# Seven-product pairs in the down-projection: a raw buffer of their own, loads two steps ahead in order, and another order of steps in the first pass

## The chip, the cores and the metric

The kernel runs on 1 core of one Trainium2 chip. The metric is device time in microseconds of one execution. The time before is 2037.37 us, the median of three runs (2033.04 to 2039.13).

## The reference, cut to what matters

The program is a two-layer decoder trunk on 256 tokens of width 2048: mixer and attention blocks, and in each layer a gated feed-forward block. The change touches the second matrix product of that block alone:

```python
def conv_ffn(h, w_up, cw, cb, w_down):
    a = h @ w_up                                  # 256 x 2048 @ 2048 x 11264
    ap = jnp.pad(a, ((0, 0), (CONV_W - 1, 0), (0, 0)))
    c = sum(ap[:, k:k + S] * cw[k] for k in range(CONV_W)) + cb
    gate, val = c[..., :D_FF], c[..., D_FF:]
    return (jax.nn.silu(gate) * val) @ w_down     # 256 x 5632 @ 5632 x 2048
```

All data is float32. TensorE multiplies a rounded type (fp32r), so each operand is split into a high part (`whi`, a rounded copy made by ScalarE) and a low part (`wlo`, the raw value less the high part, made by VectorE), and each block product is three matmuls: high by high, high by low, low by high.

## The kernel before, in words

**Groups and calls.** The 5632 hidden channels are taken in three groups of 2048, 2048 and 1536. For each of the first two groups of each layer, `gemm_seven` multiplies the hidden values of the group (2048 channels, 16 row blocks of 128) by the 2048 x 2048 piece of `w_down`. So `gemm_seven` runs four times, at 521 us, 780 us, 1482 us and 1743 us of the profiled execution.

**Passes and steps.** A call makes two passes, one for each 1024 output columns. A pass has eight steps; a step is a pair of row blocks, that is 1 MB of weights: 256 rows by 1024 columns, or four blocks of 128 x 512, b11 and b12 (the first 128 rows, left and right 512 columns), b21 and b22 (the second 128 rows). In the text steps are counted from 1 and pairs from 0, so before the change pair m stands at step m + 1 in both passes.

**Ordinary and seven-product pairs.** An ordinary pair makes 8 block products, 24 matmuls. Pairs 3 and 5 (`SEVEN`) use Winograd's form of Strassen's scheme and make 7 block products, 21 matmuls; they need four differences of weight blocks first: t1 = b12 - b11, t3 = b22 - b12, t2 = b22 - t1, t4 = b21 - t2. `differences(i, 0)` makes t1 and t3, `differences(i, 1)` makes t2 and t4. The sums of the other operand (`s7`) are made during the up-projection.

**What a step does on each engine.** `load` issues the DMAs on SP's queue into `raw` tiles of 512 KB each, of which there are 4. `prepare` makes `whi` and `wlo` of each part, by ScalarE and VectorE; an ordinary pair has 2 parts of 128 x 1024, a seven-product pair has four (before: [b11, b21] of 1024, b22 of 512, [t1, t2] and [t3, t4] of 1024). There are 4 `whi` and 4 `wlo` buffers, so a part can be made only when TensorE is through with the part that stands four parts ahead. `products` is the step's matmuls, in `three` (L290 to L292).

**Order.** Inside `gemm_seven` TensorE, ScalarE, VectorE and SP run in the order in which the code writes the instructions (`manual_schedule`); each engine takes its own queue in order and waits at the head of it. While step i is multiplied, the code writes: the first two differences of step i + 2 if that is a seven-product pair (with its load ahead of them), the parts of step i + 1 (with their load), the last two differences of step i + 2, the matmuls of step i, and up to three of the delayed additions that bring finished sums from the accumulation banks to the running total. After a seven-product pair's last step four such additions bring the Strassen sums together (four more in the three calls after the first, where the total already holds something), and four more follow each pass.

**First steps of a call.** VectorE still has work of the up-projection to finish when a call begins: two scalings, eight multiply-adds of the convolution (L828), two products `hv` and two splits `h`. They lie in its queue between the parts of the first steps.

## Time and profile before

| | |
|---|---|
| runs shown | 2033.04, 2039.13, 2037.37 us; median 2037.37 |
| the profiled execution | 2035.25 us in all, span 2033.5 us, granted TensorE clock 0.999 |
| TensorE busy | 2020.3 us, 99% of the span, 15394 matmuls |
| VectorE, ScalarE busy | 1493.2 us (73%), 1080.7 us (53%) |
| DMA | 64.7% of 16 engines' span on SP's queue, 192 GB/s of HBM traffic over the span |
| `gemm_seven`, matmuls of four calls | L290, L291 and L292, 496 each, 389 to 391 ns each, overlapped |

A matmul of 128 x 512 is shown as busy for 389 ns, but the next one starts 227 ns after it: they are pipelined. A stall of TensorE is therefore read from the starts of two following matmuls, less 0.23 us, rather than from idle time alone. In timelines a row gives start, length, engine, line and operation, then the idle time before it and what ended that.

### The profile page before, as it was taken

To read this page: it belongs to the slowest core of one execution; us is meant where nothing else is said; L and a number is where in the kernel's file an instruction comes from. 1 tells how busy PE (TensorE), PEld (TensorE's weight loads), DVE (VectorE), ACT (ScalarE), POOL (GpSimd) and SP (SyncE) were. 2 spreads that over 40 slices of the span, in tenths; PEclk is the share of its full clock that TensorE was granted. 3 is DMA by queue.
4 is the path that set the end of the run, shared out by engine and by line. 5 is a ranking of instruction groups with operands and counts; after the bars stand their busy time and mean duration, and the time that the engine had idled before them with its cause. 6 is when DMAs were issued, how large, how long until landed. Compare 5 with 4: busy or idle time off the path is not lost.

```text
span 2033.5 us, 37724 instructions
## 1 busy us (share of the span) xinstructions
PE 2020.3 (99%) x15394; PEld 1923.9 (95%) x15394; DVE 1493.2 (73%) x2064; ACT 1080.7 (53%) x1424; POOL 95.1 (5%) x131
## 2 busy tenths in 40 slices
PE   9999999999999999999999999999999999999998
PEld 8989999999889998899999999999988999889997
DVE  6866667767776777877789886777678667786675
ACT  6754644555545555445546674455544555544543
POOL 0000013000000000000052002200000000000000
PEclk9999999999999999999999999999999999999999
DMA  8675855666566665688665565578756666566654
GB/s 312 186 236 176 199 179 186 206 190 192 185 213 190 195 196 180 213 214 214 190 195 185 172 151 166 192 209 214 222 186 199 195 201 188 183 204 195 199 185 154
DMA packets 254013, 398.86 MB, mean 196 GB/s; under 512 B 65040, under 2 KB 71824, under 8 KB 253712
## 3 DMA queue, kind: packets, MB, share of 16 engines
q1 hardware_dynamic: 253264, 395.80, 64.7%
q8 instruction: 120, 1.97, 0.4%
q10 hardware_dynamic: 576, 0.66, 0.1%
q14 instruction: 53, 0.43, 0.1%
HBM read 388.01 MB, written 2.10 MB: 192 GB/s over the span
## 4 chain that ended last, share of the span: by engine, by line
PE 94%; DVE 3%; DMA 2%; issue 1%; ACT 1%; ACTq 0%; POOLq 0%; POOL 0%; DVEq 0%
PE ps L180 23%; PE ps L181 23%; PE ps L183 23%; PE ps L291 4%; PE ps L292 4%; PE ps L290 4%; PE ps L211 3%; PE ps L212 3%; PE ps L213 3%; DMA raw<-in_w_ffn_down 1%; DVE wlo L270 1%; DVE c L828 0%; ACT whi L269 0%; PE ps L714 0%; PE ps L767 0%
## 5 line engine op out<-in xcount | busy, mean ns | idle before, releaser
L144 DVE TENSOR_TENSOR wlo<-raw,whi 128x1024 fp32r<-128x1024 f32 (+1 forms) x544 | 664.3, 1238 | 396.2 <-issue 254.0
L143 ACT ACTIVATE whi<-raw 128x1024 fp32r<-128x1024 f32 (+1 forms) x544 | 569.4, 1054 | 574.1 <-PE ps L181 435.6
L180 PE MATMUL ps<-xhl,whi 128*128 128x256 f32 x3264 | 750.6, 276 | 0.0
L181 PE MATMUL ps<-xhl,whi 128*128 128x256 f32 x3264 | 750.2, 276 | 0.0
L180 PEld LDWEIGHTS ps<-xhl,whi 128*128 128x128 f32 x3264 | 612.6, 188 | 0.2
L181 PEld LDWEIGHTS ps<-xhl,whi 128*128 128x128 f32 x3264 | 612.6, 188 | 0.2
L183 PE MATMUL ps<-xhl,wlo 128*128 128x256 f32 x3264 | 403.2, 276 | 0.0
L183 PEld LDWEIGHTS ps<-xhl,wlo 128*128 128x128 f32 x3264 | 385.2, 188 | 0.0
L269 ACT ACTIVATE whi<-raw 128x1024 fp32r<-128x1024 f32 (+1 forms) x128 | 126.0, 1004 | 113.8 <-DMA raw<-in_w_ffn_down 45.8
L270 DVE TENSOR_TENSOR wlo<-raw,whi 128x1024 fp32r<-128x1024 f32 (+1 forms) x128 | 144.8, 1155 | 48.3 <-ACT whi L269 22.2
L291 PE MATMUL ps<-wlo,h 128*128 128x512 f32 x432 | 168.7, 391 | 2.5 <-DVE wlo L270 2.5
L290 PE MATMUL ps<-whi,h 128*128 128x512 f32 x432 | 168.4, 390 | 1.3 <-ACT whi L269 1.3
L292 PE MATMUL ps<-whi,h 128*128 128x512 f32 x432 | 168.2, 389 | 0.0
L828 DVE SCALAR_TENSOR_TENSOR c<-a,cT,c 128x255 f32<-128x255 f32 (+1 forms) x352 | 145.9, 477 | 0.0
L825 ACT ACTIVATE c<-a,cT 128x256 f32<-128x256 f32 x176 | 91.6, 591 | 77.4 <-DVE a L419 77.4
L180 PE MATMUL ps<-mainhl,whi 128*128 128x256 f32 x512 | 118.5, 278 | 0.0
L181 PE MATMUL ps<-mainhl,whi 128*128 128x256 f32 x512 | 118.0, 277 | 0.0
L291 PEld LDWEIGHTS ps<-wlo,h 128*128 128x128 f32 x432 | 81.1, 188 | 21.2 <-DVE wlo L270 4.4
L290 PEld LDWEIGHTS ps<-whi,h 128*128 128x128 f32 x432 | 81.1, 188 | 18.6 <-ACT whi L269 1.9
L292 PEld LDWEIGHTS ps<-whi,h 128*128 128x128 f32 x432 | 81.1, 188 | 16.8
L180 PEld LDWEIGHTS ps<-mainhl,whi 128*128 128x128 f32 x512 | 96.0, 188 | 0.1
L181 PEld LDWEIGHTS ps<-mainhl,whi 128*128 128x128 f32 x512 | 96.0, 188 | 0.1
(325 smaller groups left out, 2389.6 us busy)
## 6 DMA issues: line engine op xcount, KB each, us to landing
raw<-in_w_ffn_up SPq DMA_DIRECT2D x352, 512.0 KB, 4.2
raw<-in_w_ffn_down SPq DMA_DIRECT2D x176, 512.0 KB, 4.8
raw<-in_w_out SPq DMA_DIRECT2D x64, 512.0 KB, 4.9
raw<-in_w_in_a SPq DMA_DIRECT2D x56, 512.0 KB, 4.5
raw<-in_w_mem_kv SPq DMA_DIRECT2D x31, 512.0 KB, 5.3
raw<-in_w_in_b SPq DMA_DIRECT2D x16, 512.0 KB, 3.9
raw<-in_w_uq SPq DMA_DIRECT2D x12, 384.0 KB, 3.4
raw<-in_w_kv_a SPq DMA_DIRECT2D x8, 512.0 KB, 3.7
```

The costliest lines, as they stand in the source:

```text
L143: nc.scalar.activation(hi[:, :n], raw[:, :n], AF.Copy)
L144: nc.vector.tensor_tensor(lo[:, :n], raw[:, :n], hi[:, :n].bitcast(F32), ALU.subtract)
L180: mm(acc, wh, x[:, :S], start=first, stop=False)
L181: mm(acc, wh, x[:, S:], start=False, stop=False)
L183: mm(acc, wl, x[:, :S], start=False, stop=last)
L269: nc.scalar.activation(hi, raw, AF.Copy)
L270: nc.vector.tensor_tensor(lo, raw, hi.bitcast(F32), ALU.subtract)
L290: mm(acc, xh, wh, start=start, stop=False)
L291: mm(acc, xh, wl, start=False, stop=False)
L292: mm(acc, xl, wh, start=False, stop=stop)
L825: nc.scalar.activation(c[:, i, :], a[:, i, :], AF.Identity, scale=w(2), bias=w(3))
L828: nc.vector.scalar_tensor_tensor(o, a[:, i, : S - 2 + j], w(j), o, ALU.mult, ALU.add)
```

## The change

The seven-product pairs get a tile of their own, `raw7` (128 x 4 x 512, one buffer), and no longer use the four `raw` tiles. Their load is three DMAs in place of two: the first 128 rows with all 1024 columns (512 KB, 4 KB from each row), then two of 256 KB for b21 and b22. The tile holds b11, b12, b22, b21 in this order, so that t1 and t3 are one subtraction of 128 x 1024; t2 and t4 stay two of 128 x 512. The parts become b11 (512), [b22, b21] (1024), [t1, t3] (1024) and [t2, t4] (1024), and the products of the pair are ordered to use them in this sequence.

Loads are issued two steps ahead in the order of the steps, for all pairs. In the first pass the pairs are taken in the order 0, 1, 2, 4, 3, 6, 5, 7, so that the seven-product pairs stand at steps 5 and 7; in the second pass they stay at steps 4 and 6. Four delayed additions are allowed in a step in place of three. To make room in SBUF, masks, rotary tables and scratch squares move from a pool that lives through the whole program into one that ends before the last feed-forward block, and the transposition after the first layer uses `raw7` in place of a tile of its own.

```diff
-            prepare(0)
+            load(0)
+            load(1)
+            prepare(0)
             for i in range(len(steps)):
+                if i + 2 < len(steps):
+                    load(i + 2)
                 if seven(i + 2):
                     differences(i + 2, 0)
                 if i + 1 < len(steps):
                     prepare(i + 1)
                 if seven(i + 2):
                     differences(i + 2, 1)
-                now, later[:] = later[:3], later[3:]
+                now, later[:] = later[:4], later[4:]
                 products(i)
...
+ORDERS = ((0, 1, 2, 4, 3, 6, 5, 7), (0, 1, 2, 3, 4, 5, 6, 7))
...
         def load(i):
-            raws[i] = [self.raw_load(src(i, c)) for c in range(2)]
+            half, m = steps[i]
+            if not seven(i):
+                blocks[i] = [self.raw_load(src(i, c)) for c in range(2)]
+                return
+            raw = blocks[i] = self.tmp(sums, [P, 4, 512], "raw7", 1)
+            row = lambda j: self.rows(dn, half * 1024, 1024)(2 * m + j, 1).rearrange("p k (c n) -> p (k c) n", c=2)
+            nc.sync.dma_start(out=raw[:, 0:2, :], in_=row(0))
+            for c in range(2):
+                nc.sync.dma_start(out=raw[:, 3 - c, :], in_=row(1)[:, c, :])
 
         def differences(i, part):
+            raw = blocks[i]
             if part == 0:
-                load(i)
-                early[i] = [self.tmp(pool, [P, 4, S], "gate", 2).rearrange("p a s -> p (a s)") for _ in range(2)]
-            (b11, b21), (b12, b22) = ((raw[:, :512], raw[:, 512:]) for raw in raws[i])
-            (t1, t2), (t3, t4) = ((t[:, :512], t[:, 512:]) for t in early[i])
-            if part == 0:
-                sub(t1, b12, b11)
-                sub(t3, b22, b12)
-            else:
-                sub(t2, b22, t1)
-                sub(t4, b21, t2)
+                early[i] = [self.tmp(pool, [P, 4, S], "gate", 2).rearrange("p (a b) s -> p a (b s)", a=2) for _ in range(2)]
+                sub(early[i][0], raw[:, 1:3, :], raw[:, 0:2, :])
+                return
+            t13, t24 = early[i]
+            sub(t24[:, 0, :], raw[:, 2, :], t13[:, 0, :])
+            sub(t24[:, 1, :], raw[:, 3, :], t24[:, 0, :])
...
-            self.three(side[1], block(2 * m, 0), pick(one, 0), first, last)
-            self.three(out[0, 0], block(2 * m + 1, 0), pick(one, 1))
-            self.three(out[0, 1], s[3], pick(b22, 0))
-            self.three(side[5], s[0], pick(ta, 0), first, last)
-            self.three(side[6], s[1], pick(ta, 1), first, last)
-            self.three(side[7], s[2], pick(tb, 0), first, last)
-            self.three(out[1, 0], block(2 * m + 1, 1), pick(tb, 1))
+            self.three(side[1], block(2 * m, 0), pick(b11, 0), first, last)
+            self.three(out[0, 0], block(2 * m + 1, 0), pick(b2, 1))
+            self.three(out[0, 1], s[3], pick(b2, 0))
+            self.three(side[5], s[0], pick(t13, 0), first, last)
+            self.three(side[7], s[2], pick(t13, 1), first, last)
+            self.three(side[6], s[1], pick(t24, 0), first, last)
+            self.three(out[1, 0], block(2 * m + 1, 1), pick(t24, 1))
```

Two places show how the change moves instructions. The first is SP's queue in the first pass of the first call, from the load of the third step on. Before (`raw_757` and `raw_758` are pair 3, `raw_761` and `raw_762` pair 2, `raw_775` and `raw_776` pair 5, `raw_779` and `raw_780` pair 4):

```order
L262 DMA raw_757_6086<-in_w_ffn_down 128x2x512
L262 DMA raw_758_6088<-in_w_ffn_down 128x2x512
L262 DMA raw_761_6094<-in_w_ffn_down 128x2x512
L262 DMA raw_762_6096<-in_w_ffn_down 128x2x512
L262 DMA raw_775_6172<-in_w_ffn_down 128x2x512
L262 DMA raw_776_6174<-in_w_ffn_down 128x2x512
L262 DMA raw_779_6180<-in_w_ffn_down 128x2x512
L262 DMA raw_780_6182<-in_w_ffn_down 128x2x512
```

And the same place with the change (`raw_749` and `raw_750` are pair 2, then pair 4, pair 3 in `raw7`, pair 6, pair 5 in `raw7`, pair 7):

```order
L263 DMA raw_749_6050<-in_w_ffn_down 128x2x512
L263 DMA raw_750_6052<-in_w_ffn_down 128x2x512
L263 DMA raw_759_6090<-in_w_ffn_down 128x2x512
L263 DMA raw_760_6092<-in_w_ffn_down 128x2x512
L316 DMA raw7_765_6126<-in_w_ffn_down 128x1024
L318 DMA raw7_765_6126<-in_w_ffn_down 128x512 x2
L263 DMA raw_772_6167<-in_w_ffn_down 128x2x512
L263 DMA raw_773_6169<-in_w_ffn_down 128x2x512
L316 DMA raw7_782_6211<-in_w_ffn_down 128x1024
L318 DMA raw7_782_6211<-in_w_ffn_down 128x512 x2
L263 DMA raw_793_6253<-in_w_ffn_down 128x2x512
L263 DMA raw_794_6255<-in_w_ffn_down 128x2x512
```

The load of an ordinary pair no longer stands behind that of the seven-product pair that is multiplied after it; the load of the second seven-product pair now stands behind the parts of the first one, which hold the single `raw7`.

The second place is VectorE's queue in the second pass of the first call, from the parts of pair 3 (step 4) to the parts of pair 4 (step 5). Before:

```order
L270 TENSOR_TENSOR wlo_837_6461<-raw_826_6413,whi_836_6460 128x1024
L270 TENSOR_TENSOR wlo_839_6465<-raw_827_6415,whi_838_6464 128x512
L270 TENSOR_TENSOR wlo_841_6469<-gate_828_6417,whi_840_6468 128x1024
L270 TENSOR_TENSOR wlo_843_6473<-gate_829_6418,whi_842_6472 128x1024
L296 TENSOR_TENSOR gate_846_6504<-raw_845_6502,raw_844_6500 128x512
L296 TENSOR_TENSOR gate_847_6505<-raw_845_6502 128x512
L270 TENSOR_TENSOR wlo_851_6513<-raw_848_6508,whi_850_6512 128x1024
L270 TENSOR_TENSOR wlo_853_6517<-raw_849_6510,whi_852_6516 128x1024
```

With the change:

```order
L271 TENSOR_TENSOR wlo_836_6462<-raw7_826_6416,whi_835_6461 128x512
L271 TENSOR_TENSOR wlo_838_6466<-raw7_826_6416,whi_837_6465 128x1024
L271 TENSOR_TENSOR wlo_840_6470<-gate_827_6420,whi_839_6469 128x1024
L271 TENSOR_TENSOR wlo_842_6474<-gate_828_6421,whi_841_6473 128x1024
L297 TENSOR_TENSOR gate_844_6505<-raw7_843_6501 128x1024
L271 TENSOR_TENSOR wlo_847_6509<-raw_833_6457,whi_846_6508 128x1024
L271 TENSOR_TENSOR wlo_849_6513<-raw_834_6459,whi_848_6512 128x1024
```

The two first differences of pair 5 have become one, at the same place: behind the last part of pair 3 and ahead of both parts of pair 4. Their input, `raw7_843`, is the buffer that the first two rows read as `raw7_826`.

## The prediction

> **What bounds the kernel now.** I read the page first, then the waits of TensorE, then its timeline at those waits, then the chain that ends one of them.

> ```profile
> span 2033.5 us, 37724 instructions
> PE 2020.3 (99%) x15394; PEld 1923.9 (95%) x15394; DVE 1493.2 (73%) x2064; ACT 1080.7 (53%) x1424; POOL 95.1 (5%) x131
> ```

> TensorE is busy for 99% of the span, and the change takes no matmul away. It can gain only what TensorE loses in waits. Those for TensorE on this change's lines, summed over the whole run:

> ```profile
> PE ps L291 <- DVE wlo L270: 2.5, 4, 0.8
> PE ps L290 <- ACT whi L269: 1.3, 1, 1.3
> ```

> Five waits, all in the four calls of `gemm_seven`. Matmuls overlap, so the true loss is read from starts. TensorE's timeline at the fifth step of the first pass of each call:

> ```profile
> 541.88 0.39 PE L290 MATMUL ps<-whi,h 128*128 128x512 f32 x1
> 543.04 0.50 PE L291 MATMUL ps<-wlo,h 128*128 128x512 f32 x1 [0.76 <-DVE wlo L270]
> 543.37 0.39 PE L292 MATMUL ps<-whi,h 128*128 128x512 f32 x1
> ...
> 801.47 0.39 PE L290 MATMUL ps<-whi,h 128*128 128x512 f32 x1
> 802.22 0.50 PE L291 MATMUL ps<-wlo,h 128*128 128x512 f32 x1 [0.37 <-DVE wlo L270]
> ...
> 1503.01 0.40 PE L292 MATMUL ps<-whi,h 128*128 128x512 f32 x1
> 1504.69 0.49 PE L290 MATMUL ps<-whi,h 128*128 128x512 f32 x1 [1.28 <-ACT whi L269]
> 1505.94 0.50 PE L291 MATMUL ps<-wlo,h 128*128 128x512 f32 x1 [0.76 <-DVE wlo L270]
> ...
> 1764.71 0.40 PE L290 MATMUL ps<-whi,h 128*128 128x512 f32 x1
> 1765.71 0.50 PE L291 MATMUL ps<-wlo,h 128*128 128x512 f32 x1 [0.60 <-DVE wlo L270]
> ```

> The undisturbed distance of two starts is 0.23 us (front part), so the waits cost 1.16 - 0.23 = 0.93, 0.75 - 0.23 = 0.52, 1.45 + 1.02, and 0.77 us. The matmul after a wait starts 0.33 us on (543.04 to 543.37), which adds 0.10 to each call. Sum: 0.93 + 0.52 + 2.47 + 0.77 + 0.40 = **5.1 us**. What is late there, by the chain that ended last:

> ```profile
> 535.21 5.35 DMA raw<-in_w_ffn_down
> ...
> 541.76 1.23 DVE wlo L270
> 543.00 0.04 issue
> 543.04 0.50 PE ps L291
> ```

> Pair 4's first DMA is issued at 535.21 only, lands at 540.56, and its `wlo` is ready at 542.99, 0.05 us before TensorE starts. It was issued late because it stood on SP's queue behind pair 5's load.

> **The change part by part.** *Removed: the late load.* With loads in the order of the steps and pair 4 moved to step 4, an ordinary pair waits for its own `raw` tiles alone, which come free two ordinary pairs earlier. The step that comes fifth is now pair 3, whose `raw7` is empty at the start of a call, so its three DMAs go out directly behind pair 4's. VectorE's leftover of the up-projection is over by then:

> ```profile
> 524.20 3.23 DVE L828 SCALAR_TENSOR_TENSOR c<-a,cT,c 128x255 f32<-128x255 f32 x8
> ```

> It ends near 527.4, fourteen us ahead of the step that stalls. I take all 5.1 us as removed.

> *Added: a wait for the single `raw7`.* Pair 5 can be loaded only when the last reader of pair 3 in `raw7` is through, the `wlo` of [b22, b21]. Its first difference stands on VectorE ahead of both parts of the ordinary pair in between (step 6 of the first pass, step 5 of the second). If the load is late, those two `wlo` wait behind it, and TensorE waits for the first of them at its second matmul. That is eight places, two in each call. Timing of the second pass of the first call, before the change:

> ```profile
> 575.08 0.63 ACT L269 ACTIVATE whi<-raw 128x512 fp32r<-128x512 f32 x1 [1.52 <-PE ps L292]
> 577.85 1.06 ACT L269 ACTIVATE whi<-gate 128x1024 fp32r<-128x1024 f32 x1 [2.13 <-PE ps L292]
> 581.66 1.23 DVE L270 TENSOR_TENSOR wlo<-gate,whi 128x1024 fp32r<-128x1024 f32 x1 [1.49 <-ACT whi L269]
> 582.80 0.69 DVE L296 TENSOR_TENSOR gate<-raw,raw 128x512 f32<-128x512 f32 x1
> 584.01 2.35 DVE L270 TENSOR_TENSOR wlo<-raw,whi 128x1024 fp32r<-128x1024 f32 x2
> 585.30 0.47 PE L291 MATMUL ps<-wlo,h 128*128 128x512 f32 x1
> 585.62 0.39 PE L292 MATMUL ps<-whi,h 128*128 128x512 f32 x1
> ```

> The second part's `whi` starts at 575.08, when TensorE releases its buffer. The new second part is 1024 wide: 575.08 + 1.06 + 0.06 + 1.23 (the `wlo`) = 577.43, and SP issues at 577.45. Call D the time from there until the third DMA has landed. Then 0.10 until VectorE starts (a transfer landing at 540.56 was used at 540.66), 1.14 for the one difference of 1024 (the distance of two 1024-wide operations, 582.80 less 581.66), 1.23 for the `wlo`, 0.05 to TensorE: 2.52 us. TensorE wants it at 585.30. The stall is 577.45 + D + 2.52 - 585.30 = D - 5.33, and with the restart of 0.10, **D - 5.23**. With D below 5.2 VectorE would start the difference at 582.80, as now, and there is no stall: 582.80 + 1.14 + 1.23 + 0.05 = 585.22. The present 0.09 us (585.62 - 585.30 - 0.23) would go too; over the calls some 0.2 us.

> In the second passes of the three later calls additions to the total lie between:

> ```profile
> 835.77 1.82 DVE L270 TENSOR_TENSOR wlo<-raw,whi 128x1024 fp32r<-128x1024 f32 x2
> 844.51 0.47 PE L291 MATMUL ps<-wlo,h 128*128 128x512 f32 x1
> ```

> The same two widths end at 837.59 there. A fourth addition in that step adds 0.60, the earlier loads take back up to 1.0: 836.6 to 838.2, and I take 837.3. The stall is then 837.3 + 0.02 + D + 2.52 - 844.51 + 0.10 = **D - 4.57**. In the first passes nothing but parts and differences stands in VectorE's queue at this point, so they are priced like the first call's second pass: five places of the first kind, three of the second.

> *What is D?* No row has the three DMAs. The nearest are two of 512 KB issued 0.6 us apart (issues at 837.01 and 837.62, then the time from issue to landing of each, then the second of two other such pairs, issued at 848.95 and 589.45):

> ```profile
> 837.01 0.37 SPq L262 DMA_DIRECT2D raw<-in_w_ffn_down  x1
> 837.62 0.37 SPq L262 DMA_DIRECT2D raw<-in_w_ffn_down  x1
> raw<-in_w_ffn_down SPq DMA_DIRECT2D x1, 512.0 KB, 4.0
> raw<-in_w_ffn_down SPq DMA_DIRECT2D x1, 512.0 KB, 5.8
> raw<-in_w_ffn_down SPq DMA_DIRECT2D x1, 512.0 KB, 6.2
> raw<-in_w_ffn_down SPq DMA_DIRECT2D x1, 512.0 KB, 5.2
> ```

> So a megabyte is complete 6.4, 6.8 and 5.8 us after its first issue. Low end: the third DMA is issued 1.2 us after the first, and a DMA that comes first in line takes 4.0, so 5.2. High end 6.8. I take **6.0**, between the pairs of 5.8 and 6.4, since little else is in flight then and half of `raw7` comes in rows of 4 KB.

> [...]

> *Hidden parts.* One difference in place of two saves 1.21 - 1.14 = 0.07 us of VectorE, inside the stall formula. Sixteen more DMA issues lie on SP, which mostly waits for buffers. Four additions in a step add 0.6 us to VectorE, which has gaps; the accumulation banks that they release are wanted a whole step later. The moved pools change addresses only.

> **The sum.** -5.3 + 5 x (6.0 - 5.23) + 3 x (6.0 - 4.57) = -5.3 + 3.85 + 4.3 = +2.9 us. The profiled execution took 2035.25, which gives 2038.1. That execution lies 2.1 us under the median shown; from the median it would be 2040.2. I say 2039, between them.

> **The rivals.**

> *In time.* D is at most 5.2. For it: the transfers are few at that moment, and half the bytes come in larger rows. Against it: all three pairs quoted are slower. At 5.2 the first five places are free, the others cost 3 x 0.63 = 1.9, so the net is -3.4; below 4.6 it is the full -5.3: 2032 to 2034 from the median. Still within 0.3%.

> *Clearly slower: the transfers behind.* With loads in order, the next ordinary pair's two DMAs go out directly behind the three of `raw7`. If the five share the engines, D grows. From D = 6.4 on the eight stalls sum to 8 x 6.4 - 39.9 = 11.3, net +6.0, which is 0.3%; at 6.8 they are 14.5, net +9.2, some 2046. For it: two of the three pairs already stand at or above 6.4 without followers. [...]

> *The old stall stays* because something else is late at step 5, VectorE's backlog for one. Then 5.1 us is not won and the new stalls come on top: +8 us, 2045. Against it: the chain shows the DMA, not VectorE, as the last to arrive, and 14 us lie between.

> **How the numbers follow.** Late `raw7` with D from 5.2 to 6.4: 0.60, its own range -3.4 to +6, 2033 to 2043. In time: 0.16. Clearly slower by D over 6.4: 0.20. Old stall stays: 0.04. The range that holds 8 in 10 reaches from the full gain seen from the profiled execution, 2031, to 2047. What a measurement can tell from no change is about 0.3%, 6.1 us, and more than all the waits that can be removed: faster 0.07 (only by chance of the runs or a gain that no row shows), slower 0.25, same 0.68.

> **What would show it.** The wait of L291 at the fifth step of the first pass must be gone. If I am right, L291 waits for `wlo` at the first matmuls of step 6 of the first pass and step 5 of the second, about 0.8 us each, longer in the second passes of the last three calls, and VectorE's chain there goes back through the difference (L297) to a DMA into `raw7`. If `raw7`'s last DMA lands within 5.2 us of the first issue, there is no such wait and the rival holds. I am wrong if the eight places are clean, or if TensorE waits elsewhere in the calls.

## The result, and the profile after

The changed kernel takes 2050.98 us (median of 4 runs, 2050.30 to 2054.80) against 2035.80 us for the kernel before (4 runs, 2033.04 to 2039.13). The ratio is 1.0078, with an interval of 1.0057 to 1.0099: slower by some 15 us, outside the predicted range. The profiled execution took 2050.56 us. The head of its page:

```profile
span 2048.8 us, 37725 instructions
PE 2026.4 (99%) x15394; PEld 1927.7 (94%) x15394; DVE 1491.7 (73%) x2048; ACT 1083.5 (53%) x1424; POOL 95.1 (5%) x131
```

The span grew by 15.3 us at a granted clock of 0.995 (before: 0.999). VectorE is even 1.5 us less busy. What changed is in the waits, first TensorE's, then VectorE's (in total, times, longest):

```profile
PE ps L292 <- DVE wlo L271: 12.9, 8, 4.5
DVE gate L297 <- DMA raw<-in_w_ffn_down: 24.8, 16, 4.7
```

The five old waits are gone. Eight new ones have come, two in each `gemm_seven`, and VectorE waits at the first difference (L297) for a load. TensorE's timeline at step 6 of the first pass (the first and the last of four calls), then at step 5 of the second pass (all four calls):

```profile
547.25 0.39 PE L291 MATMUL ps<-whi,h 128*128 128x512 f32 x1
548.06 0.50 PE L292 MATMUL ps<-wlo,h 128*128 128x512 f32 x1 [0.43 <-DVE wlo L271]
...
1781.03 0.40 PE L291 MATMUL ps<-whi,h 128*128 128x512 f32 x1
1781.81 0.50 PE L292 MATMUL ps<-wlo,h 128*128 128x512 f32 x1 [0.38 <-DVE wlo L271]
...
584.69 0.39 PE L291 MATMUL ps<-whi,h 128*128 128x512 f32 x1
585.81 0.50 PE L292 MATMUL ps<-wlo,h 128*128 128x512 f32 x1 [0.73 <-DVE wlo L271]
...
844.90 0.39 PE L291 MATMUL ps<-whi,h 128*128 128x512 f32 x1
848.45 0.50 PE L292 MATMUL ps<-wlo,h 128*128 128x512 f32 x1 [3.15 <-DVE wlo L271]
...
1551.67 0.40 PE L291 MATMUL ps<-whi,h 128*128 128x512 f32 x1
1556.55 0.80 PE L292 MATMUL ps<-wlo,h 128*128 128x512 f32 x1 [4.49 <-DVE wlo L271]
1557.15 0.63 PE L293 MATMUL ps<-whi,h 128*128 128x512 f32 x1
1557.57 0.63 PE L291 MATMUL ps<-whi,h 128*128 128x512 f32 x1
...
1818.66 0.40 PE L291 MATMUL ps<-whi,h 128*128 128x512 f32 x1
1821.88 0.80 PE L292 MATMUL ps<-wlo,h 128*128 128x512 f32 x1 [2.82 <-DVE wlo L271]
```

By the distance of starts less 0.23 us, the first five places lose 0.58, 0.59, 0.67, 0.55 and 0.89 us, 3.3 in all. The last three lose 3.32, 4.65 and 2.99 us, 11.0 in all. Behind each of these three the matmuls start 0.43 us apart instead of 0.23 for a while (1557.15 to 1557.57). Stretches of 3.41 us, the time for which the half clock lasts in call 2 (848.86 to 852.28), show why (us, busy time of PE, PEld, DVE, ACT and POOL, granted clock, DMA share, GB/s):

```profile
845.45:848.86 3.41, 0.41 (x2) 0.37 (x3) 2.83 (x3) 1.06 (x1) 0.00 (x0) 1.00 0.63 222
848.86:852.28 3.42, 3.42 (x10) 2.65 (x9) 3.38 (x5) 0.00 (x0) 0.00 (x0) 0.50 0.63 192
...
1552.01:1555.42 3.41, 0.06 (x1) 0.00 (x0) 1.28 (x2) 1.06 (x1) 0.00 (x0) 1.00 0.73 271
1555.42:1558.83 3.41, 2.28 (x5) 1.82 (x6) 3.38 (x4) 0.00 (x0) 0.00 (x0) 0.50 0.33 86
1558.83:1562.25 3.42, 3.42 (x9) 2.64 (x8) 1.87 (x3) 0.60 (x1) 0.00 (x0) 0.50 0.61 227
...
1818.25:1821.66 3.41, 0.81 (x4) 0.33 (x2) 2.20 (x2) 1.06 (x1) 0.00 (x0) 1.00 0.66 242
1821.66:1825.07 3.41, 3.19 (x8) 2.52 (x9) 3.38 (x6) 0.00 (x0) 0.00 (x0) 0.50 0.52 154
```

The granted clock falls to one half for exactly one or two such stretches, which begin within 1.2 us of the wait's end (before it in calls 3 and 4). Half of TensorE's busy time in them is lost, as an estimate from the clock of 0.50: (3.42 + 2.28 + 3.42 + 3.19) / 2 = 6.2 us. With 3.3, 11.0 and some 0.5 of restarts that is 21.0 us, and less the 5.1 us of old waits 15.9, against the 15.3 us by which the span grew. Nothing of size is left to explain.

Why the three are long is on VectorE. Its timeline in the second pass of call 2:

```profile
830.50 1.22 DVE L297 TENSOR_TENSOR gate<-raw 128x1024 f32<-128x1024 f32 x1 [1.74 <-DMA raw<-in_w_ffn_down]
831.64 2.35 DVE L271 TENSOR_TENSOR wlo<-raw,whi 128x1024 fp32r<-128x1024 f32 x2
833.91 1.41 DVE L297 TENSOR_TENSOR gate<-raw,gate 128x512 f32<-128x512 f32 x2
835.24 2.47 DVE L298 TENSOR_TENSOR total<-total,ps 128x512 f32<-128x512 f32 x4
837.63 1.82 DVE L271 TENSOR_TENSOR wlo<-raw,whi 128x512 fp32r<-128x512 f32 x2
...
846.03 1.23 DVE L297 TENSOR_TENSOR gate<-raw 128x1024 f32<-128x1024 f32 x1 [3.32 <-DMA raw<-in_w_ffn_down]
```

and SP's queue at the release of `raw7` (L316 and L318 are its loads, L263 an ordinary one), in the first pass of call 1 and the second passes of calls 2, 3 and 4:

```profile
539.64 0.34 SPq L316 DMA_DIRECT2D raw<-in_w_ffn_down  x1
...
839.48 0.34 SPq L316 DMA_DIRECT2D raw<-in_w_ffn_down  x1
...
840.82 9.10 SPq L263 DMA_DIRECT2D raw<-in_w_ffn_down  x4
...
1546.24 0.34 SPq L316 DMA_DIRECT2D raw<-in_w_ffn_down  x1
...
1812.33 0.34 SPq L316 DMA_DIRECT2D raw<-in_w_ffn_down  x1
```

VectorE loses 1.74 us at 830.50 already, because the first load of `raw7` in the pass is late too; then come two parts, two differences and four additions, so the `wlo` of [b22, b21] is through at 839.45 only. The load goes out at 839.48. VectorE then stands idle for 3.32 us up to 846.03, with both `wlo` of the ordinary pair behind the difference, and TensorE waits for the first of them. The differences that end this wait in the other three places:

```profile
545.64 1.23 DVE L297 TENSOR_TENSOR gate<-raw 128x1024 f32<-128x1024 f32 x1 [0.59 <-DMA raw<-in_w_ffn_down]
...
1554.14 1.23 DVE L297 TENSOR_TENSOR gate<-raw 128x1024 f32<-128x1024 f32 x1 [4.75 <-DMA raw<-in_w_ffn_down]
...
1819.46 1.22 DVE L297 TENSOR_TENSOR gate<-raw 128x1024 f32<-128x1024 f32 x1 [3.08 <-DMA raw<-in_w_ffn_down]
```

From the first issue to the start of the difference (D and 0.1 us) it is 6.0 us in call 1, but 6.55, 7.90 and 7.13 us in calls 2 to 4.

One sum gives every wait: that time, plus 2.42 us for the difference, one `wlo` and the step to TensorE, less the time by which the issue lies ahead of the matmul that waits. In the first pass of call 1 this is 6.00 + 2.42 - 7.84 = 0.58 us, in the second passes of calls 2 to 4 it is 6.55 + 2.42 - 5.65 = 3.32, 7.90 + 2.42 - 5.66 = 4.66 and 7.13 + 2.42 - 6.56 = 2.99. It holds to 0.02 us at all eight places here, and at those of the four edits below that leave the difference ahead of the parts (39 of the 40 places wait; at the other the sum is negative).

### The profile page after: what moved, and what is told of

It is laid out like the page before. It is cut to its first block, busy times and chain, and to the rows that moved or that the text cites. A ratio compares the mean times of both kernels' runs of the same rounds, so it can differ in the third digit from the quotient of the medians.

```text
span 2048.8 us, 37725 instructions
## 1 busy us (share of the span) xinstructions
PE 2026.4 (99%) x15394; PEld 1927.7 (94%) x15394; DVE 1491.7 (73%) x2048; ACT 1083.5 (53%) x1424; POOL 95.1 (5%) x131
## 4 chain that ended last, share of the span: by engine, by line
PE 92%; DMA 3%; DVE 3%; issue 1%; ACT 1%; SPq 0%; POOLq 0%; DVEq 0%; POOL 0%; ACTq 0%
PE ps L181 23%; PE ps L182 23%; PE ps L184 23%; PE ps L292 4%; PE ps L293 4%; PE ps L291 3%; DMA raw<-in_w_ffn_down 3%; PE ps L212 3%; PE ps L214 3%; PE ps L213 3%; DVE wlo L271 2%; ACT whi L270 0%; PE ps L724 0%; PE ps L723 0%; PE ps L726 0%
## 5 line engine op out<-in xcount | busy, mean ns | idle before, releaser
L270 ACT ACTIVATE whi<-raw 128x1024 fp32r<-128x1024 f32 (+1 forms) x128 | 128.7, 1007 | 108.0 <-PE ps L293 64.9
L292 PE MATMUL ps<-wlo,h 128*128 128x512 f32 x432 | 171.5, 397 | 12.9 <-DVE wlo L271 12.9
L291 PE MATMUL ps<-whi,h 128*128 128x512 f32 x432 | 170.5, 395 | 0.0
L293 PE MATMUL ps<-whi,h 128*128 128x512 f32 x432 | 170.3, 394 | 0.0
L292 PEld LDWEIGHTS ps<-wlo,h 128*128 128x128 f32 x432 | 82.6, 191 | 33.3 <-DVE wlo L271 16.4
L291 PEld LDWEIGHTS ps<-whi,h 128*128 128x128 f32 x432 | 82.3, 191 | 17.5
## 6 DMA issues: line engine op xcount, KB each, us to landing
raw<-in_w_ffn_up SPq DMA_DIRECT2D x352, 512.0 KB, 4.3
raw<-in_w_ffn_down SPq DMA_DIRECT2D x160, 512.0 KB, 4.9
raw<-in_w_out SPq DMA_DIRECT2D x64, 512.0 KB, 4.8
raw<-in_w_in_a SPq DMA_DIRECT2D x56, 512.0 KB, 4.5
raw<-in_w_mem_kv SPq DMA_DIRECT2D x31, 512.0 KB, 4.9
raw<-in_w_in_b SPq DMA_DIRECT2D x16, 512.0 KB, 4.2
```

The source lines that it names most:

```text
L270: nc.scalar.activation(hi, raw, AF.Copy)
L291: mm(acc, xh, wh, start=start, stop=False)
L292: mm(acc, xh, wl, start=False, stop=False)
L293: mm(acc, xl, wh, start=False, stop=stop)
```

## The experiments

My theory: the first difference stands ahead of the ordinary pair's parts on VectorE and waits there for `raw7`; the release of `raw7` and D set the length. Rivals: VectorE is simply late (additions, backlog), whatever the difference waits for; the transfers behind lengthen D; one late load in the second pass starts it all. Each verdict compares with runs of the kernel before on the same chip.

**The difference behind the parts** (both differences of step i + 2 written behind the parts of step i + 1):

```diff
-                if seven(i + 2):
-                    differences(i + 2, 0)
                 if i + 1 < len(steps):
                     prepare(i + 1)
                 if seven(i + 2):
+                    differences(i + 2, 0)
                     differences(i + 2, 1)
```

> The changed kernel with one thing moved: the first difference of a seven-product pair stands on VectorE behind both parts of the ordinary pair, no longer ahead of them. Theory (VectorE's head waits for raw7 and holds up parts whose data is there): the eight waits of L292 go (16.4 us of lost starts and the slow matmuls behind three of them), all four calls come within 0.5 us of undisturbed, time 2030 to 2032 us, under the kernel before. Rival (raw7's single buffer is the cost wherever the difference stands): the waits move one step on, to the seven-product step itself, and stay at 1 to 4 us each, time 2045 us or more.

Measured: 2030.33 us against 2034.16, ratio 0.9979 (0.9970 to 0.9987). This beats both kernels, by 3.8 and some 20 us. The first line of its page, and VectorE in the second pass of call 2:

```profile
span 2028.2 us, 37725 instructions
...
840.09 2.35 DVE L271 TENSOR_TENSOR wlo<-raw,whi 128x1024 fp32r<-128x1024 f32 x2
843.73 1.22 DVE L297 TENSOR_TENSOR gate<-raw 128x1024 f32<-128x1024 f32 x1 [1.29 <-DMA raw<-in_w_ffn_down]
```

The difference still waits 1.29 us for its load, but the two `wlo` are through ahead of it, and TensorE has no wait in these calls. The place in VectorE's queue is what costs, not the late load as such. The span is 5.3 us below that of the kernel before, which is the old stall and no more.

**The order of pairs alone** (the kernel before with the new order of the first pass; loads, buffers, differences and three additions a step as before):

```diff
-        steps = [(half, m) for half in range(2) for m in range(n)]
+        steps = [(half, m) for half, order in enumerate(ORDERS) for m in order]
```

> The kernel before with the new order of steps in the first pass alone (0, 1, 2, 4, 3, 6, 5, 7); loads, raw tiles and differences as before. Theory (a seven-product pair at step 4 comes too early after the up-projection, the order alone heals it): the wait at the fifth step of the first pass goes in all four calls and no new one appears, 5 us less than before, 2030 to 2032 us. Rival (the load of pair 3 ahead of pair 4 on SP's queue is the cost at any step): a wait of 0.5 to 2.5 us for wlo stays at step 4 or 6 of the first pass, time as before within 2 us.

Measured: 2036.76 us, ratio 1.0013 (1.0004 to 1.0021). Neither expectation holds in full. The old stall is gone, by the order alone; but TensorE now waits in the second passes of calls 2 to 4, here call 2:

```profile
839.90 0.39 PE L293 MATMUL ps<-whi,s 128*128 128x512 f32 x1
841.40 0.47 PE L291 MATMUL ps<-whi,s 128*128 128x512 f32 x1 [1.11 <-DVE total L298]
```

The first seven-product pair of the pass needs an accumulation bank that VectorE's additions have not emptied: 1.50 - 0.23 = 1.27 us in each of three calls, and some 0.4 us at the next step.

**Four additions in a step, without `raw7`** (the same with the limit of four):

```diff
-                now, later[:] = later[:3], later[3:]
+                now, later[:] = later[:4], later[4:]
```

> The kernel before with two parts of the change alone: the new order of pairs in the first pass, and four delayed additions in a step in place of three. No raw7, the loads and the differences as before. With the order alone TensorE waited for additions in the second passes of the three later calls (1.25 us at the fourth step and 0.35 to 0.4 us at the fifth), 6.6 us over undisturbed cadence in four calls. Theory (three additions in a step come too late for the accumulation banks under the new order, a fourth mends that): these waits go, the old stall of the first pass stays away, and with 5 to 6 us of waits less than the kernel before the time is 2029 to 2031 us, as the version with the differences behind. That would mean that raw7 and the loads two steps ahead bring nothing. Rival (the waits for additions come of something else, VectorE's work of the new order): 2035 to 2037 us with the waits in place.

Measured: 2032.76 us against 2033.86, ratio 0.9994 (0.9985 to 1.0003). The waits for additions are gone, as the theory had it, yet the time is not the 2029 to 2031 expected. Three waits remain at step 5 of the second passes, here by TensorE's waits and ScalarE's timeline in call 2:

```profile
PE ps L292 <- DVE wlo L271: 2.2, 3, 0.8
...
842.98 1.06 ACT L270 ACTIVATE whi<-raw 128x1024 fp32r<-128x1024 f32 x1 [2.16 <-DMA raw<-in_w_ffn_down]
```

There the ordinary pair's own load comes late. The faster version, with loads in order and `raw7`, has no such wait; so something in it beyond the order and the fourth addition brings the rest. The two kernels differ in `raw7`, in the order of the loads and in the place of the differences, and the runs do not separate these.

**Three additions in the faster version** (the first experiment's kernel with the limit of three):

```diff
-                now, later[:] = later[:4], later[4:]
+                now, later[:] = later[:3], later[3:]
```

> The faster version (the changed kernel with the first differences behind the next pair's parts) with three delayed additions in a step, as in the kernel before, in place of four. Theory as above: TensorE waits for additions in the second passes of the three later calls again, some 1.2 to 1.7 us each, 4 to 5 us in all: 2034 to 2036 us. Rival (in the changed kernel VectorE is ahead enough for three a step, and four were not needed there): 2030 us.

Measured: 2034.55 us, ratio 1.0001 (0.9992 to 1.0010), with the same 1.3 us at the same three places. The fourth addition is needed; without it the faster version's gain is gone.

**The additions left out** (the changed kernel without the four additions to the total in calls 2 to 4; the output lacks these sums):

```diff
-            if not fresh:
+            if False:
```

> The changed kernel without the four additions that bring the Strassen sums into the running total in calls 2 to 4 (that part of the output is left out; the first call has none). Theory (VectorE's queue ahead of the second part of pair 3 is what releases raw7 late in these calls): step 5 of the second pass costs 0.7 to 2.3 us there, no slow matmuls, time about 2038 us. Rival (additions lie in gaps, the late load alone counts): the waits stay at 3 us and more, time 2049 us or more.

Measured: 2039.74 us, ratio 1.0029 (1.0018 to 1.0039). In call 2 the load now goes out 7.88 us ahead of the matmul that waits (837.65 to 845.30 + 0.23), where it was 5.65 us; it takes 0.40 us longer, and the wait falls from 3.32 to 1.48 us (the distance of starts less 0.23). SP and VectorE in call 2:

```profile
837.65 0.34 SPq L316 DMA_DIRECT2D raw<-in_w_ffn_down  x1
...
844.60 1.23 DVE L297 TENSOR_TENSOR gate<-raw 128x1024 f32<-128x1024 f32 x1 [1.49 <-DMA raw<-in_w_ffn_down]
```

In call 3 the issue moves from 5.66 to 7.98 us ahead and in call 4 from 6.56 to 7.33; the waits are 0.29 and 1.43 us in place of 4.65 and 2.99. About half of these two gains is a shorter D (by 2.05 and 0.78 us), which nothing in the edit explains. In the profiled execution no stretch of half clock is left in the calls. The five short waits stay (0.56 to 0.73 us), so the additions lengthen the waits and do not make them; calling VectorE "simply late" doesn't explain the rest.

**The first load of the second pass a step earlier** (the late load at 830.50, moved ahead of pair 2's load):

```diff
-                if i + 2 < len(steps):
+                if i + 3 == heavy[1][0]:
+                    load(i + 3)
+                if i + 2 < len(steps) and i + 2 != heavy[1][0]:
```

> The changed kernel with the second pass's first raw7 load (pair 3) issued one step earlier, ahead of the load of pair 2. Theory (in the later calls this load, landing after 8 us behind two megabytes, delays the first difference, all that follows on VectorE, and so the release of raw7): the first difference of pair 3 waits no more, the wait at step 5 of the second pass falls from 3.3, 4.7 and 3.0 to about 1.6, 2.9 and 2.1 us in calls 2 to 4, the slow matmuls behind it go, time about 2041 us. Rival (the release is set by the parts and additions, not by this load): waits and time stay within 1 us of the changed kernel.

Measured: 2046.29 us, ratio 1.0064 (1.0041 to 1.0087), the four runs between 2042.35 and 2055.12. In the profiled one (2049.03) that first difference waits for nothing, but the ordinary load that it has overtaken is now late, and the long waits are 3.53, 1.29 and 4.67 us. Only in call 3 does `raw7`'s second load go out earlier (7.54 us ahead of the matmul in place of 5.66); in call 2 it is as before and in call 4 later. In that execution the edit moves the lateness more than it removes it. But the granted clock was 0.999 in the runs of 2042.35 and 2043.55 us, near the 2041 expected, and 0.996 and 0.995 in the other two; as only one of the four has a trace, the question stays open. The first passes, which the edit leaves alone, also differ here (1.45 and 1.09 us in calls 1 and 2 against 0.58 and 0.59): so one and the same wait differs by up to 0.9 us between two executions.

**The parts in another order** ([b22, b21] made and multiplied ahead of b11):

```diff
-                raws = [raws[:, 0, :], flat(raws[:, 2:4, :])] + [flat(t) for t in early.pop(i)]
+                raws = [flat(raws[:, 2:4, :]), raws[:, 0, :]] + [flat(t) for t in early.pop(i)]
```

> The changed kernel with the parts of a seven-product pair made and multiplied in another order: [b22,b21] first, b11 behind it. The last reader of raw7 that the next seven-product load waits for is then done earlier, by one first part's work on VectorE, 1.1 us (two wlo of 512 columns at about 0.6 us); raw7's other reader is b11's, and it is now the later one, but it is short. Theory (the second load of raw7 waits for its release, and its first difference blocks VectorE): every one of the eight waits shortens by the time by which the release moves. If the release moves by the 1.1 us, the five short ones (0.55 to 0.89 us) go to nothing and the three long ones (2.99 to 4.66 us) become 1.9 to 3.6 us, some of them without slow matmuls behind: 2040 to 2046 us. If b11's parts only change places with the others and the release stays where the last of the four parts is done, nothing changes: 2050 us. Rival (VectorE is simply late there, whoever holds raw7): 2050 us with the release earlier.

Measured: 2051.92 us, ratio 1.0091 (1.0070 to 1.0112), as the changed kernel. The release came no earlier in the second passes (840.29 in call 2), since the last reader of `raw7` is now b11's part: the edit did not move it the way that it was meant to. In the second passes of calls 2 to 4 the load goes out 0.55 to 1.85 us later against TensorE, and the waits of 3.90, 3.42 and 3.59 us follow by the sum above. Whether a second `raw7` tile would free the load was not tried.

**Nothing behind `raw7`'s second load** (the ordinary load that followed it goes ahead of it):

```diff
+        second = {h[1] for h in heavy}
...
+                if i + 2 in second:
+                    load(i + 3)
-                if i + 2 < len(steps):
+                if i + 2 < len(steps) and i + 1 not in second:
```

> The changed kernel with one ordinary load (the two DMAs that followed directly behind the second seven-product load of a pass on SP's queue) put ahead of that load. Nothing follows the three DMAs of raw7 then. Theory (transfers queued behind lengthen the ones ahead): the time from the first issue to the third landing, 5.9 to 6.4 us where nothing else was late, falls towards 5.0 to 5.4 us, and the five short waits (0.55 to 0.89 us) to 0.3 us or nothing; the three long ones shorten by as much, where their length comes of the release as well: 2041 to 2047 us. Rival (the three DMAs take their 5.9 to 6.4 us by themselves, or the load that is now ahead of them costs as much): waits as in the changed kernel or longer, 2050 us or more.

Measured: 2043.36 us, ratio 1.0049 (1.0034 to 1.0064), the time that the theory expected. In call 3 the first issue to the difference takes 5.27 us in place of 7.90:

```profile
1547.77 0.34 SPq L317 DMA_DIRECT2D raw<-in_w_ffn_down  x1
...
1553.04 1.23 DVE L297 TENSOR_TENSOR gate<-raw 128x1024 f32<-128x1024 f32 x1 [2.20 <-DMA raw<-in_w_ffn_down]
```

The wait falls by as much, from 4.65 to 2.11 us. Between issue and landing the DMA engines moved 1.05 MB (5.17 us at 203 GB/s), `raw7`'s own; in the changed kernel it was 1.86 MB (7.80 us at 239 GB/s), so 0.8 MB of the load behind went ahead of `raw7`'s last piece. Place by place the waits are not as expected: of the long ones call 4's falls as well (2.99 to 1.26 us), while call 2's stays at 3.24, since its load goes out 0.5 us later; of the five short ones two go (0.2 us or less), and three grow to 1.02, 1.28 and 1.55 us. At these three the load ahead was issued 3.1 to 3.7 us before `raw7`'s, and the first issue to the difference takes 6.35 to 6.95 us; but at the two that go, with such a load 3.5 us ahead, it takes 5.33 and 5.70. What sets it there is not shown.

**A ladder of waits** (the faster version with needless VectorE work of 6 to 20 operations ahead of ordinary parts, the output unchanged):

```diff
+                for _ in range(IDLE.get((self.calls, i + 1), 0)):
+                    nc.vector.tensor_tensor(self.idle, self.x[:, 0, :], self.x[:, 0, :], ALU.subtract)
```

> The kernel without stalls (differences behind the next pair's parts), with 6 to 20 needless VectorE subtractions of 256 columns put ahead of an ordinary pair's parts, at two places in each of the four gemm_seven calls; the output is as before. They make TensorE wait at eight places for lengths spread between nothing and about 6 us, with no other change to VectorE's order and no DMA moved. Theory (the waiting itself makes TensorE slow afterwards): stalls up to 1.7 us, as in the first passes of the changed kernel, are followed by matmuls every 227 ns; stalls of about 3 us and more, as in its later second passes (2.99, 3.31, 4.66 us), are followed by matmuls every 427 ns, for some 3 to 5 us. Rival (the slow matmuls come of something else that happens at those places, the late load of raw7 or the bank that the next matmul takes): no slow matmuls after any of these stalls, or after short ones as well.

Measured (one execution, 2066.83 us): a wait of 2.45 us leaves the clock alone, waits of 4.13, 4.54 and 8.21 us halve it for one, one and three stretches of 3.41 us. So idle time alone does it; the rival falls. But length alone does not decide: the kernel with the parts in another order has a wait of 3.59 us with no slow matmul behind, while 2.99 us was enough in the changed kernel and 3.24 us in the one with nothing behind `raw7`'s load. Each with stretches cut at that run's own edges, which every fall and rise of the clock in it shares. First the ladder (2.45 us, its later and idler stretch and the one after; then 4.13 us), then the wait of 3.59 us, then that of 3.24 us:

```profile
1808.60:1812.02 3.42, 1.79 (x8) 1.47 (x9) 3.40 (x5) 0.21 (x1) 0.00 (x0) 1.00 0.21 33
1812.02:1815.43 3.41, 3.41 (x17) 2.80 (x16) 3.41 (x5) 0.63 (x1) 0.00 (x0) 1.00 0.75 265
...
859.70:863.11 3.41, 0.00 (x0) 0.00 (x0) 3.24 (x8) 0.89 (x2) 0.00 (x0) 1.00 0.00 0
863.11:866.52 3.41, 3.32 (x8) 2.64 (x9) 3.41 (x5) 0.00 (x0) 0.00 (x0) 0.50 0.66 192
...
1817.52:1820.93 3.41, 1.64 (x8) 1.00 (x6) 0.75 (x1) 0.77 (x1) 0.00 (x0) 1.00 0.91 309
1820.93:1824.34 3.41, 1.75 (x8) 1.43 (x9) 3.38 (x5) 0.81 (x2) 0.00 (x0) 1.00 0.52 192
1824.34:1827.75 3.41, 3.41 (x16) 2.81 (x15) 3.41 (x4) 1.07 (x1) 0.00 (x0) 1.00 0.72 253
...
847.25:850.66 3.41, 1.37 (x6) 1.16 (x7) 3.41 (x4) 0.66 (x1) 0.00 (x0) 1.00 0.05 13
850.66:854.07 3.41, 3.41 (x10) 2.63 (x9) 2.74 (x4) 0.83 (x1) 0.00 (x0) 0.50 0.84 282
```

In these traces a stretch at full clock in which TensorE is busy for 1.39 us or less of 3.41 is followed by one at half clock; 1.64 us or more is not (1.39 is call 2 of the kernel with the first load a step earlier, and inside the calls no stretch of the eleven traces lies between). The wait of 3.59 us fell across an edge: it left 1.64 and 1.75 us busy in its two stretches, and the clock stayed at 1.00.

## Why the prediction was wrong, point by point

- **The bound, and the old stall: right.** Only waits moved the time, and the stall at the fifth step of the first pass is gone in all four calls. My reason for it was too narrow: the order of the pairs heals it even with the loads as before.
- **The added wait: right in mechanism and in all eight places.** The experiment with the difference behind the parts shows the mechanism.
- **The five places of the first kind: right in size.** Predicted 0.77 us each with the restart, 3.85 in all; measured 3.3 and some 0.5 of restarts. D was 5.9 to 6.3 us there, as taken; what the rows of 4 KB do to it no run shows.
- **The three places of the second kind: here it failed.** The step is the sentence "836.6 to 838.2, and I take 837.3" and the formula D - 4.57 with D = 6.0 (836.6, besides, left out the fourth addition that 838.2 has): 1.33 us of wait each (1.43 with the restart), 4.0 in all, against 11.0 measured. About half of the missing 7.0 us is the release. In call 2 I had the load issued 7.19 us ahead of the matmul that waits (837.32 to 844.51); it went out 5.65 us ahead (839.48, that matmul being wanted at 844.90 + 0.23), so 1.5 us later, and the same arithmetic gives 1.5 and 0.6 in calls 3 and 4: 3.7 us. I had subtracted up to 1.0 for earlier loads, where the first `raw7` load in fact lands late, behind 2 MB of ordinary loads issued just ahead (in call 2 four DMAs from 817.36 on, then its own from 821.35 on, and the difference can start at 830.50), and blocks VectorE by the very wait that I had described for the second. The other 3.2 us is D: 6.4, 7.8 and 7.0 in place of 6.0. In the last two of these 1.86 and 1.64 MB landed before `raw7` was complete, in the first pass of call 1 1.42. Why more of the load behind goes ahead there is not shown, and in part it looks like chance: with the same load behind, D at these three places was 5.8 to 7.8 us in the changed kernel and three of its edits (additions left out, earlier first load, parts in another order).
- **The clock: missing.** No term stood for what a wait does to the matmuls after it: 6.2 us. The rows that I had read of before have no wait over 1.5 us and no half clock. The end of that trace does show one: TensorE does nothing from 2026.17 to 2029.58 us, and the granted clock is 0.50 from there on. A wait of 1.3 us, as I had predicted, leaves about 2.1 us of a stretch busy, or more (3.41 less 1.3, an estimate), where stretches with 1.64 us busy kept the full clock; the wait of 2.99 us left 0.81 us busy in the stretch from 1818.25 and halved it.
- **Hidden parts: wrong in one.** I let VectorE's gaps hide the fourth addition here, though the release above counts its 0.60 us. It lies in the queue ahead of the release, where leaving four additions out brings the release forward by 0.8 to 2.3 us against the matmul. And I had not seen that the new order needs it, which two experiments show: 1.3 us at each of three places without it.
- **The rivals.** "Clearly slower: the transfers behind" came nearest: without followers D was 5.2 to 5.9 us in the second passes of calls 2 to 4. But the followers were there at the five short places too, with D as I had taken it. I gave it 0.20 and priced it to 2046 at D = 6.8, with the release still early and the clock full. The old stall did not stay, and no load was in time. The chance of slower, 0.25, was too low: the three places share their release and D, so that an error in either counts three times.

## What to carry to other kernels

VectorE takes its queue in order and passes a late operand on to all that stands behind it: in call 2 its wait of 3.32 us for one load (846.03) became 3.32 us of TensorE's, while 1.29 us with the difference behind the parts (843.73) became none. Place work that waits for a fresh load behind the work that TensorE needs next. When a single buffer is reused, walk its release back through every wait of the releasing engine, since one late load (1.74 us of VectorE's time at 830.50) delays the release of the next. A wait of TensorE should be priced with the clock behind it: waits up to 2.45 us were paid once here, those of 2.99 us and more mostly 1.3 to 1.8 times (an estimate: the wait and half of TensorE's busy time at the clock of 0.50 behind it, as shares of the wait), the one of 3.59 us once.

## What the hardware showed beyond what I expected

A stretch at half clock in which TensorE was idle for a third (1555.42, 2.28 us busy) was followed by a second one; after 3.18 us or more (3.18 behind the ladder's wait of 4.54 us) the clock came back. Counted at the granted clock of 0.50 (the starts are 0.43 us apart there, in place of 0.23) these are, as an estimate, 1.14 and 1.59 us of work at full clock: one limit between 1.39 and 1.59 us of work in a stretch fits every fall and rise of the eleven traces inside the calls. It is read from them and was not tested apart.

On SP's queue transfers issued behind a load can lengthen it: in call 3 the same three DMAs to one tile took 5.2 us with none behind and 7.8 us with a megabyte issued in the 1.8 us after the first of them, of which 0.8 MB landed ahead of the tile's last piece. These are the extremes: over the eight places, from the first issue to the difference, it was 5.3 to 7.0 us without followers and 6.0 to 7.9 us with them.
